# P times the softmax factors: one GpSimd instruction per attention step in place of four

## The chip, the core and the metric

The kernel runs on one core of a Trainium2 chip. A core has a matrix engine (TensorE, PE in the profile, with its weight loads as PEld), a vector engine (VectorE, DVE), an activation engine (ScalarE, ACT), a general engine (GpSimd, POOL), and SyncE (SP), which here only starts transfers. Each engine works through its own list of instructions in order; they wait for each other through semaphores. The metric is the device time in microseconds (us) of one execution.

## The reference

One layer of a streaming encoder, for 512 positions of width 1024, all in float32: a SwiGLU feed-forward block, a mixer with two branches (a gated linear recurrence, and attention in a sliding window), and a second feed-forward block, each between two RMS norms. What the change touches is the softmax of the attention, with 16 query heads in 4 groups of 4, and a learned sink per head that counts in the sum but has no value:

```
sc = einsum('bnqgrd,bnkgd->bngrqk', qc, kband) * HEAD_DIM ** -0.5
sc = sc + bias
sc = where(valid, sc, NEG_INF)
p  = softmax(concatenate([sc, sink], axis=-1), axis=-1)[..., :-1]
o  = einsum('bngrqk,bnkgd->bnqgrd', p, vband)
```

Everything after the projections of q, k and v and before the projection `w_attn_out` belongs to it. A query attends to its own chunk of 64 keys and to the two chunks before.

## The kernel before, in words

Every float32 product is made of three: operands are split into a high part that TensorE multiplies exactly enough (`whi`, `PH`, uT part 0) and a rest (`wlo`, `PL`, uT part 1), and high x high, rest x high and high x rest are added up in the accumulator. The splitting is work for ScalarE (high part, L178 and L213) and VectorE (rest, L179 and L214: a subtraction of 128x1024 elements for each block of weights, with both inputs in on-chip memory). Blocks of weights are loaded by SP in the order of one list (`order`), split a few blocks ahead, and used by `mm_feat` (L223 to L225), 24 matmuls a unit.

The order of the work is written out by hand. `mm_feat` calls `point()` twice a unit; `point()` counts up and emits what has come due, and `later(n, fn, rank)` puts a piece of work n points ahead. So the attention is woven between the units of matmuls in the stage from about 530 to 672 us: units of the q projection (`wq`), of the recurrent branch's output (`lru`) and of the gates (`wg`), listed in `att_units`.

There are 16 attention steps, 4 groups of heads `g` times 4 blocks of 128 queries `j`, started every 2.2 points (`ATT_STEP`). A step goes through five pieces, `ATT_LAG` points apart:

- `att_s` (L1292, L1293): TensorE makes the scores of four heads, 128 queries x 256 keys each (128 keys where j = 0).
- `scores` (L1298 to L1302): VectorE adds the bias, takes the row maximum, and writes the tile P (`pt`), 128 partitions (queries) x 4 heads x 256 columns.
- `exps` (L1306, L1307): ScalarE takes exponentials of P in place, one instruction a head, which also gives the sums `d`, 128x4; and the exponential of the sink.
- `factors` (L1309 to L1314): VectorE adds sink and sum and takes the reciprocal (L1310, L1311), so `d` holds a factor for each query and head; GpSimd multiplies P by it in place (L1313).
- `att_t` (L1329): TensorE transposes P, four blocks of 128x128 for j = 0 and eight otherwise, into PSUM (`pt`); ScalarE and VectorE split that into `PH` and `PL` (L213, L214); `att_o` (L1345, L1346) multiplies by v, and the output is put together by L1354 or L1356, L1360, L1364 and, on GpSimd, L1365.

Beside L1313 and L1365, GpSimd's list in this stage holds the loading of the bias tiles (L1274 to L1276) and, twice, the sums of weight blocks for the gates' last units (L543, L544, L538, L539), which use fewer products at the price of sums. The functions that the change touches:

Of the kernel before, what the change touches and what calls it, by code (L numbers as in the profile page):

```python
# [13 lines left out]
ALU = mybir.AluOpType  # L14

P = 128
# [35 lines left out]
def hybrid_layer(ctx: ExitStack, tc: tile.TileContext, a: dict, out: bass.AP):  # L52
    nc = tc.nc
    act, dve, pool, pe, sp = nc.scalar, nc.vector, nc.gpsimd, nc.tensor, nc.sync
# [8 lines left out]
    def slot(shape, dt=F32, name="s"):  # L63
        uid[0] += 1
        return sb.tile(shape, dt, tag="slot", name=f"{name}_{uid[0]}")

    def bank(name="ps"):
        uid[0] += 1
        return pp.tile([P, 512], F32, tag="ps", name=f"{name}_{uid[0]}")

    def small(w, name="m", bufs=4):
        uid[0] += 1
        return sm.tile([P, w], F32, tag=f"sm{w}", name=f"{name}_{uid[0]}", bufs={1: 11, 4: 12}.get(w, bufs))
# [123 lines left out]
    def later(n, fn, rank=1):  # L197
        uid[0] += 1
        due.append((now[0] + n, rank, uid[0], fn))
# [1078 lines left out]
    def att_s(g, j):  # L1278
        n = 256 if j else 128
        k0 = (j - 1) * P if j else 0  # L1280
        b0 = 256 - n
        pt = slot([P, 4, 256], name="P")
        m, ng, d, es = (small(4, x) for x in ("m", "ng", "d", "es"))
        sk = vec[:, V_SINK + 4 * g : V_SINK + 4 * g + 4]
        pss = []
        for hp in range(2):
            ps = bank("s")
            for hh in range(2):
                x = 2 * hp + hh
                o = ps[:, hh * 256 : hh * 256 + n]  # L1290
                lq = QS[2 * g + x // 2][:, x % 2, j * P : (j + 1) * P]
                pe.matmul(o, lq, KS[g][:, 0, k0 : k0 + n], start=True, stop=False)  # L1292
                pe.matmul(o, lq, KS[g][:, 1, k0 : k0 + n], start=False, stop=True)  # L1293
            pss.append(ps)

        def scores():
            for x in range(4):
                dve.tensor_tensor_reduce(  # L1298
                    out=pt[:, x, b0:256], in0=pss[x // 2][:, (x % 2) * 256 : (x % 2) * 256 + n], in1=BT[g][:, x, b0:256],
                    scale=1.0, scalar=sk[:, x : x + 1], op0=ALU.add, op1=ALU.max, accum_out=m[:, x : x + 1])  # L1300
            dve.tensor_scalar(out=ng, in0=m, scalar1=-1.0, scalar2=None, op0=ALU.mult)
            dve.tensor_tensor(out=es, in0=sk, in1=m, op=ALU.subtract)  # L1302

        def exps():
            for x in range(4):
                act.activation(pt[:, x, b0:256], pt[:, x, b0:256], AF.Exp, bias=ng[:, x : x + 1], accum_out=d[:, x : x + 1])  # L1306
            act.activation(es, es, AF.Exp)  # L1307

        def factors():  # L1309
            dve.tensor_tensor(out=d, in0=d, in1=es, op=ALU.add)  # L1310
            dve.reciprocal(d, d)  # L1311
            for x in range(4):
                pool.tensor_scalar(out=pt[:, x, b0:256], in0=pt[:, x, b0:256], scalar1=d[:, x : x + 1], scalar2=None, op0=ALU.mult)  # L1313
            at[(g, j)] = pt  # L1314

        later(ATT_LAG[0], scores, 0)
        later(ATT_LAG[0], exps, 2)
        later(ATT_LAG[1], factors, 3)
        later(ATT_LAG[2], lambda: att_t(g, j))

    def att_t(g, j):
        pt = at.pop((g, j))
        kts = (0, 1) if j else (1,)
        PH = slot([P, 2, 512], F32R, name="PH")
        PL = slot([P, 2, 512], F32R, name="PL")
        pss = [bank("pt") for _ in kts]
        for ps, kt in zip(pss, kts):
            for x in range(4):
                pe.transpose(ps[:, x * P : (x + 1) * P], pt[:, x, kt * P : (kt + 1) * P], ident)  # L1329
        def out():  # L1330
            for ps, kt in zip(pss, kts):
                split2(PH[:, kt, :], PL[:, kt, :], ps)

        later(ATT_LAG[3], out)
        later(ATT_LAG[4], lambda: att_o(g, j, PH, PL, kts))
# [217 lines left out]
```

## Time and profile before

| What | Value |
|---|---|
| Median of 3 runs | 1129.06 us (1128.47 to 1129.76) |
| Profiled execution | 1128.72 us, its span 1126.9 us |
| Granted TensorE clock | 0.999 |
| GpSimd busy | 369.0 us, 33% of the span |
| VectorE busy | 838.4 us, 74% |
| TensorE busy | 1117.2 us, 99% |

A row of a group of instructions names line, engine, operation, output<-inputs, shapes and count, then busy us and mean ns of one, then the idle time of the engine just before them with what ended it. A row of the order of time gives start (us from the span's start), length and the instruction, and in brackets the idle time before it and what ended that. A row of waits names the waiting instruction, the releaser, and us in total, times and the longest. In a row of one line's instructions stand the shortest, the median and the longest duration in ns, then the first and the last start. A row of busy time in a stretch gives for each engine busy us and, in brackets, the count of instructions. A profile records matmuls overlapping each other, since they are pipelined.

### The profile page before, as it was taken

The page shows a single profiled execution, that of the slowest core. Times are in us where ns is not written, and L with a number is a line of the kernel's source. Part 1 is how long each engine was busy: PE and PEld are TensorE (multiplying, and loading weights), DVE is VectorE, ACT ScalarE, POOL GpSimd, SP SyncE. Part 2 cuts the span into 40 slices and gives each one's busy share as a digit, 9 for nine tenths or more (in the row PEclk, how much of TensorE's full clock was granted, in tenths as well). Part 3 has the DMA queues.
Part 4 walks back from the last instruction along what each step waited for, and adds up shares of the span by engine and source line. Part 5 has one row for each costly group of instructions (what it writes and reads, how often), then busy time and mean ns, then how long its engine had stood idle before and what let it go on. Part 6 is the DMA issues. An engine that isn't in the chain of part 4 may idle for free.

```text
span 1126.9 us, 18141 instructions
## 1 busy us (share of the span) xinstructions
PE 1117.2 (99%) x7054; PEld 1012.9 (90%) x7054; DVE 838.4 (74%) x1238; ACT 623.4 (55%) x1114; POOL 369.0 (33%) x286
## 2 busy tenths in 40 slices
PE   9999999999999999999999999999999999999997
PEld 7899999988889977899888888889999999998886
DVE  5889989886436998887778877767898777975313
ACT  7755555574325778666656664456555555564211
POOL 0044444200000523242655863000966566700000
PEclk9999999999999999999999999999999999999999
DMA  9226563265314653156223235521333332255101
GB/s 337 108 82 149 136 129 113 76 224 168 98 53 148 157 118 102 38 171 241 60 91 113 92 134 186 211 90 38 113 107 92 102 113 86 88 199 170 40 19 56
DMA packets 40310, 136.54 MB, mean 121 GB/s; under 512 B 4880, under 2 KB 6800, under 8 KB 40224
## 3 DMA queue, kind: packets, MB, share of 16 engines
q1 hardware_dynamic: 36432, 123.28, 32.9%
q0 software_dynamic: 3504, 11.58, 5.3%
q8 instruction: 55, 0.90, 0.3%
q10 hardware_dynamic: 288, 0.52, 0.2%
q14 instruction: 31, 0.25, 0.1%
HBM read 121.74 MB, written 11.53 MB: 118 GB/s over the span
## 4 chain that ended last, share of the span: by engine, by line
PE 94%; DVE 2%; ACT 1%; POOL 1%; DMA 1%; issue 1%; DVEq 0%; SPq 0%; POOLq 0%; ACTq 0%
PE c L492 13%; PE c L493 13%; PE c L494 13%; PE acc L243 8%; PE acc L242 8%; PE acc L241 8%; PE f L223 8%; PE f L224 8%; PE f L225 8%; ACT P L1306 1%; DVE P L1298 1%; PE pt L1329 1%; PE tr L333 1%; DVE wlo L179 1%; PE f L849 1%
## 5 line engine op out<-in xcount | busy, mean ns | idle before, releaser
L492 PE MATMUL c<-uT,whi 128*128 128x256 f32 x528 | 149.8, 284 | 0.0
L494 PE MATMUL c<-uT,whi 128*128 128x256 f32 x528 | 149.7, 284 | 0.0
L493 PE MATMUL c<-uT,wlo 128*128 128x256 f32 x528 | 149.7, 283 | 0.0
L493 PE MATMUL c<-Xh,wlo 128*128 128x256 f32 x504 | 143.0, 284 | 0.0
L492 PE MATMUL c<-Xh,whi 128*128 128x256 f32 x504 | 143.0, 284 | 0.0
L241 PE MATMUL acc<-whi,hT 128*128 128x512 f32 x352 | 137.3, 390 | 0.0
L242 PE MATMUL acc<-wlo,hT 128*128 128x512 f32 x352 | 137.1, 390 | 0.0
L243 PE MATMUL acc<-whi,hT 128*128 128x512 f32 x352 | 137.1, 390 | 0.0
L223 PE MATMUL f<-uT,whi 128*128 128x512 f32 (+1 forms) x376 | 134.4, 358 | 0.0
L224 PE MATMUL f<-uT,wlo 128*128 128x512 f32 (+1 forms) x376 | 133.0, 354 | 0.0
L225 PE MATMUL f<-uT,whi 128*128 128x512 f32 (+1 forms) x376 | 133.0, 354 | 0.0
L214 DVE TENSOR_TENSOR wlo<-S,whi 128x1024 fp32r<-128x1024 f32 x88 | 129.1, 1466 | 5.1 <-ACT whi L213 4.2
L494 PE MATMUL c<-Xl,whi 128*128 128x256 f32 x456 | 129.3, 284 | 0.0
L213 ACT ACTIVATE whi<-S 128x1024 fp32r<-128x1024 f32 x88 | 90.4, 1054 | 25.8 <-DVE S L539 22.0
L493 PEld LDWEIGHTS c<-uT,wlo 128*128 128x128 f32 x528 | 101.5, 192 | 0.1
L492 PEld LDWEIGHTS c<-uT,whi 128*128 128x128 f32 x528 | 101.5, 192 | 0.1
L494 PEld LDWEIGHTS c<-uT,whi 128*128 128x128 f32 x528 | 101.5, 192 | 0.0
L492 PEld LDWEIGHTS c<-Xh,whi 128*128 128x128 f32 x504 | 96.9, 192 | 0.3 <-issue 0.3
L493 PEld LDWEIGHTS c<-Xh,wlo 128*128 128x128 f32 x504 | 96.9, 192 | 0.1
L494 PEld LDWEIGHTS c<-Xl,whi 128*128 128x128 f32 x456 | 87.7, 192 | 0.0
L223 PEld LDWEIGHTS f<-uT,whi 128*128 128x128 f32 x376 | 71.2, 189 | 10.9 <-issue 1.6
L225 PEld LDWEIGHTS f<-uT,whi 128*128 128x128 f32 x376 | 71.2, 189 | 9.8
(380 smaller groups left out, 2890.3 us busy)
## 6 DMA issues: line engine op xcount, KB each, us to landing
raw_w2a<-in_w2a_dram SPq DMA_DIRECT2D x22, 512.0 KB, 4.1
raw_w1b<-in_w1b_dram SPq DMA_DIRECT2D x22, 512.0 KB, 4.2
raw_w3b<-in_w3b_dram SPq DMA_DIRECT2D x22, 512.0 KB, 4.2
raw_w2b<-in_w2b_dram SPq DMA_DIRECT2D x22, 512.0 KB, 4.2
raw_w3a<-in_w3a_dram SPq DMA_DIRECT2D x21, 512.0 KB, 4.4
raw_w1a<-in_w1a_dram SPq DMA_DIRECT2D x20, 512.0 KB, 4.3
raw_wg<-in_wg_dram SPq DMA_DIRECT2D x16, 512.0 KB, 3.9
raw_xr<-in_xr_dram SPq DMA_DIRECT2D x8, 512.0 KB, 4.0
```

The source lines that it names most:

```text
L179: dve.tensor_tensor(out=lo, in0=r, in1=f32(hi), op=ALU.subtract)
L213: act.activation(hi, src, AF.Copy)
L214: dve.tensor_tensor(out=lo, in0=src, in1=f32(hi), op=ALU.subtract)
L223: pe.matmul(ps[:, c0:c1], wh[:, s], h_, start=k == 0, stop=False)
L224: pe.matmul(ps[:, c0:c1], wl[:, s], h_, start=False, stop=False)
L225: pe.matmul(ps[:, c0:c1], wh[:, s], l_, start=False, stop=k == KT - 1)
L241: pe.matmul(acc[n], x[:, 0, c], wh[:, s], start=first, stop=False)
L242: pe.matmul(acc[n], x[:, 0, c], wl[:, s], start=False, stop=False)
L243: pe.matmul(acc[n], x[:, 1, c], wh[:, s], start=False, stop=last)
L492: pe.matmul(ps, wh[:, s], xh, start=first, stop=False, skip_group_check=True)
L493: pe.matmul(ps, wl[:, s], xh, start=False, stop=False, skip_group_check=True)
L494: pe.matmul(ps, wh[:, s], xl, start=False, stop=k == 3, skip_group_check=True)
```

## The change

In `factors`, the loop of four GpSimd instructions, each of which multiplies one head's 128x256 (or 128x128) block by a column of `d`, is replaced by one two-operand multiplication over all four heads. Its second operand is `d` with a third dimension of step 0, so that each of a query's four factors is read again for each of the n columns of its head (n = 256, or 128 where j = 0). The multiplied numbers and their place are the same. The order of all instructions on the five engines stays, except that each group of four on GpSimd is now one, so 64 instructions become 16.

```diff
         def factors():
             dve.tensor_tensor(out=d, in0=d, in1=es, op=ALU.add)
             dve.reciprocal(d, d)
-            for x in range(4):
-                pool.tensor_scalar(out=pt[:, x, b0:256], in0=pt[:, x, b0:256], scalar1=d[:, x : x + 1], scalar2=None, op0=ALU.mult)
+            p_ = pt[:, :, b0:256]
+            pool.tensor_tensor(out=p_, in0=p_, in1=d.unsqueeze(2).to_broadcast([P, 4, n]), op=ALU.mult)
             at[(g, j)] = pt
```

A transpose on TensorE waits for the instruction on GpSimd that wrote its part of P: before, each head's transposes could start after that head's multiplication; now those of all four heads start after the one.

## The prediction

> **What bounds the kernel now.** I read the page first (busy shares, then the chain of work that ended last), then busy time by stretch for the attention stage, the waits in it, and the order of time of each engine there.
>
> ```profile
> PE 1117.2 (99%) x7054; PEld 1012.9 (90%) x7054; DVE 838.4 (74%) x1238; ACT 623.4 (55%) x1114; POOL 369.0 (33%) x286
> ...
> PE 94%; DVE 2%; ACT 1%; POOL 1%; DMA 1%; issue 1%; DVEq 0%; SPq 0%; POOLq 0%; ACTq 0%
> ```
>
> TensorE is busy for 1117.2 of 1126.9 us and carries 94% of the chain. GpSimd (POOL) carries 1%. The changed lines run only in the attention stage, from 530 to 672 us:
>
> ```profile
> core 0: us, PE busy (x) PEld busy (x) DVE busy (x) ACT busy (x) POOL busy (x), PEclk, DMA share, GB/s
> 530.00:672.00 142.00, 140.90 (x765) 121.20 (x764) 109.49 (x297) 87.26 (x233) 93.18 (x106) 1.00 0.31 97
> ```
>
> There TensorE stands idle 142.00 - 140.90 = 1.10 us at a granted clock of 1.00; VectorE (DVE) has 142.00 - 109.49 = 32.5 us to spare, GpSimd 48.8. So no more than about 1.1 us of visible idle time can be won in this stage. The waits say whose it is:
>
> ```profile
> POOL P L1313 <- DVE d L1311: 24.4, 8, 4.4
> ...
> DVE d L1310 <- ACT es L1307: 16.3, 12, 2.2
> ...
> PEld pt L1329 <- POOL P L1313: 1.5, 2, 0.8
> ...
> PE pt L1329 <- POOL P L1313: 1.1, 2, 0.6
> ```
>
> All of it, 1.1 us in two waits, is TensorE's transposes (L1329) waiting for the multiplications by the softmax factors (L1313). GpSimd itself mostly waits for VectorE's reciprocal (L1311). Each step's slack is the distance from the start of its multiplications on GpSimd to its first transpose on TensorE:
>
> ```profile
> 537.39 2.37 POOL L1313 TENSOR_SCALAR P<-P,d 128x128 f32<-128x128 f32 x4
> 543.11 4.67 POOL L1313 TENSOR_SCALAR P<-P,d 128x256 f32<-128x256 f32 x4 [3.35 <-ACT whi L178]
> 549.74 4.23 POOL L1313 TENSOR_SCALAR P<-P,d 128x256 f32<-128x256 f32 x4 [1.97 <-DVE d L1311]
> ...
> 632.33 4.59 POOL L1313 TENSOR_SCALAR P<-P,d 128x256 f32<-128x256 f32 x4
> ...
> 655.29 3.63 POOL L1313 TENSOR_SCALAR P<-P,d 128x256 f32<-128x256 f32 x4 [3.97 <-DVE d L1311]
> ...
> 664.82 4.70 POOL L1313 TENSOR_SCALAR P<-P,d 128x256 f32<-128x256 f32 x4
> ```
>
> ```profile
> 541.04 0.60 PE L1329 MATMUL pt<-ident,P 128*128 128x128 f32 x4
> ...
> 547.90 1.04 PE L1329 MATMUL pt<-ident,P 128*128 128x128 f32 x8
> ...
> 554.73 1.03 PE L1329 MATMUL pt<-ident,P 128*128 128x128 f32 x8
> ...
> 635.95 0.49 PE L1329 MATMUL pt<-ident,P 128*128 128x128 f32 x3
> 636.97 0.76 PE L1329 MATMUL pt<-ident,P 128*128 128x128 f32 x5 [0.53 <-POOL P L1313]
> ...
> 659.47 1.03 PE L1329 MATMUL pt<-ident,P 128*128 128x128 f32 x8
> ...
> 668.45 0.56 PE L1329 MATMUL pt<-ident,P 128*128 128x128 f32 x3
> 669.58 0.77 PE L1329 MATMUL pt<-ident,P 128*128 128x128 f32 x5 [0.57 <-POOL P L1313]
> ```
>
> The slacks are 3.65, 4.79, 4.99, 3.62, 4.18 and 3.63 us for the steps that start at 537, 543, 549, 632, 655 and 664 (the ten others have more). In the two that wait, TensorE did three transposes and stood before the fourth head's, for 0.53 and 0.57 us.
>
> **The change part by part.** *Removed:* 64 multiplications by a column of factors, four per step.
>
> ```profile
> L1313 POOL TENSOR_SCALAR P<-P,d 128x256 f32<-128x256 f32 x48 | 51.5, 1090 | 35.9 <-DVE d L1311 23.2 <-ACT PH L213 5.8 <-ACT es L1307 3.6
> ...
> L1313 POOL TENSOR_SCALAR P<-P,d 128x128 f32<-128x128 f32 x16 | 12.3, 778 | 1.3 <-DVE d L1311 1.2
> ```
>
> That is 51.5 + 12.3 = 63.8 us of GpSimd time: 12 full steps of about 4.3 us and four half-width ones of about 3.1 us.
>
> *Added:* 16 two-input multiplications, 12 of 128x1024 and 4 of 128x512 elements, whose second operand repeats one factor along 256 (or 128) columns. No row has such a repeated operand. The nearest are the two-input operations with plain operands:
>
> ```profile
> 636.88 0.72 POOL L1365 TENSOR_TENSOR OL<-o,OH 128x256 fp32r<-128x256 f32 x1
> ...
> 627.46 1.28 POOL L544 TENSOR_TENSOR S<-S,raw_wg 128x512 f32<-128x512 f32 x1
> ...
> L1170 POOL TENSOR_TENSOR xf<-xf,xf x4: 2412/3267/3279, 366.4 to 375.6; 128x1024 f32<-128x1024 f32 x4
> ...
> L544 POOL TENSOR_TENSOR S<-S,raw_w1a x8: 1622/2158/3448, 56.8 to 200.1; 128x512 f32<-128x512 f32 x8
> ...
> L176 POOL CAST whi<-raw_wg 128x1024 fp32r<-128x1024 f32 x6 | 6.8, 1257 | 22.5 <-PE i L1112 8.3 <-PE f L224 8.0 <-DVE xc_t L1128 6.2
> ```
>
> 0.72, 1.28 and 2.41 us for 256, 512 and 1024 elements lie on a line of 2.2 ns per element. I take 2.41 us for a full step and 1.28 for a half one, because shape, type and engine are the same and only the step of one operand differs. The lower end is a one-input pass over 128x1024, 1.26 us (if the repeated factor cost no reading); the upper end is twice the slowest two-input row of 128x512, 2 x 3.448 = 6.9 us. At my value GpSimd's work goes from 63.8 to 12 x 2.41 + 4 x 1.28 = 34.0 us, nearly all of it beside TensorE's work.
>
> The Trainium skill, "GPSIMD Engine Reference", section 4.1, speaks against the change: two-input elementwise work is about 2x slower than VectorE's there, while one-input work runs at roughly line rate. Estimated from its 1.2 GHz, four one-input passes of 256 columns would be 0.85 us, and its 2.6 cycles per element make one two-input pass of 1024 about 2.2 us, a loss of 1.4 us per step; 2.2 us is still under every slack, so the sum would be the same by it. The trace bears out the second figure and not the first: the fastest plain rows above are near 2.2 ns per element with two inputs, and the one-input multiplications average 1.09 us for 256.
>
> *Moved on the path.* TensorE's first transpose of a step used to need the first head only, now it needs all four; what counts is the slack against the single instruction. 2.41 is under every slack, by 1.21 us in the tightest step (3.62). Even if the instruction at 632 starts about 1 us late behind a VectorE operation, as the first of the four there did, 3.4 us is under 3.62. Both waits go: -0.53 - 0.57 = -1.10 us. What is late next in these two steps is TensorE's own queue.
>
> *Nothing new is queued in front of others:* order and count of GpSimd's other instructions, of its bias loads and of SP's transfers stay. Behind the multiplication on GpSimd stand the subtractions of L1365 and the weight sums of L538 to L544; they start up to 2 us earlier, which frees ScalarE's buffers sooner, worth nothing while TensorE has no other idle time in the stage. The adding up of the sums and the reciprocal (L1310, L1311) stay on VectorE at no change.
>
> *The price on VectorE.* A long two-input GpSimd instruction and a VectorE operation with two SBUF inputs do not run together:
>
> ```profile
> 366.38 12.46 POOL L1170 TENSOR_TENSOR xf<-xf,xf 128x1024 f32<-128x1024 f32 x4 [11.82 <-ACT xf L350]
> ```
>
> ```profile
> 373.15 3.42 DVE L1059 TENSOR_TENSOR rglo<-rgraw,rghi 128x1024 fp32r<-128x1024 f32 x1
> ...
> 550.15 1.23 DVE L179 TENSOR_TENSOR wlo<-raw_wq,whi 128x1024 fp32r<-128x1024 f32 x1 [0.58 <-ACT whi L178]
> ...
> 578.52 1.23 DVE L179 TENSOR_TENSOR wlo<-raw_lru,whi 128x1024 fp32r<-128x1024 f32 x1 [0.63 <-ACT whi L178]
> ...
> L179 DVE TENSOR_TENSOR wlo<-raw_lru,whi x7: 1214/1226/1227, 535.4 to 610.6; 128x1024 fp32r<-128x1024 f32 x7
> L179 DVE TENSOR_TENSOR wlo<-raw_wq,whi x5: 1218/1226/1227, 530.1 to 587.7; 128x1024 fp32r<-128x1024 f32 x5
> L179 DVE TENSOR_TENSOR wlo<-raw_wg,whi x4: 1218/1442/2310, 614.5 to 640.2; 128x1024 fp32r<-128x1024 f32 x4
> ```
>
> Beside L1170 a subtraction of 128x1024 takes 3.42 us; beside the four short multiplications (550.15 lies inside the series 549.74 to 553.97) it takes its plain 1.23 and the series is stretched instead. With one instruction of 2.41 us from 549.74 the subtraction of 550.15 would wait until 552.15, 2.0 us. There are 16 such subtractions in the stage. I take nine as held for 2.0 us, 18 us of VectorE time against 32.5 us to spare, about 2 per step, so I cost it at nothing for TensorE. The cover is VectorE's idle time; if it is gone, what follows is the second rival. Ends: 0 held, and all 16 by 3.42 - 1.23 = 2.2, 35 us.
>
> **The sum:** 1128.72 - 1.10 = 1127.6 us, against the profiled execution's own time (1128.72, of which 1126.9 are its span); this execution lies 0.34 us under the median of the runs shown, 1129.06. The case's own range is 1127.2 to 1129.5: the lower end adds that the weight loads waited 1.5 us, 0.4 more than the matmuls, the upper end lets the held VectorE operations bring back about 2 us. 0.2%, 2.26 us, is about what a measurement of this kernel can tell from no change.
>
> **Rivals.** *1. The repeated operand is read slowly (slower).* For it: no row shows it, and worst two-input rows run at 6.7 ns per element. Against it: the line of 2.2 ns through three sizes. With D the length of a full-width instruction, TensorE waits max(0, D - slack) in the steps at 543, 549, 632, 655 and 664. At D = 4.9: 0.11 + 0 + 1.28 + 0.72 + 1.27 = 3.4, less the 1.10 won, +2.3; from there it decides. At D = 6.0: 1.21 + 1.01 + 2.38 + 1.82 + 2.37 = 8.8, +7.7, 1136.4 us, or more, since steps of longer slack are left out. At 6.9 the same sum gives 13.3, +12.2, 1140.9 us.
>
> *2. VectorE held for the whole instruction becomes the bound (slower).* For it: 3.42 against 1.23 above, and from 0 to 35 us of holding against 32.5 us of spare time. Against it: in 12 of the 16 steps VectorE waits for ScalarE's last exponentials before L1310 (16.3 us), and can catch up there. If a third of the 18 us is not caught up, 6 us arrive at the transposes: 1127.6 + 6 = 1133.6 us. It decides once 3.4 us arrive. The Trainium skill, "SBUF — State Buffer", section "Who interferes with whom", states the same as a rule: the pair of ports that VectorE shares with GpSimd is an exclusive lock, held for a whole instruction, and a VectorE instruction with two SBUF inputs contends with a GpSimd one that reads SBUF. The rows of L1170 and L1059 agree; the short multiplications, beside which the subtraction kept its 1.23 us, do not show the block.
>
> *3. No gain: the two waits stay.* Step 632 starts behind a weight sum and a VectorE operation; if the instruction runs at 3.27 us, as three of the four of L1170 did, and 1 us late, it ends at 636.6, and TensorE waits as before: 1128.7 us.
>
> *4. More than the waits is won* (1126.0 us): GpSimd free 30 us sooner would have to speed up work outside the two waits, of which the idle time of TensorE in this stage shows none.
>
> **How the numbers follow.** Forecast 0.44, rival 3 0.13, together the same (within 0.2%): 0.57. Rival 1 0.20, rival 2 0.17: slower 0.37. Rival 4 0.06: faster. The likeliest is 1127.6. The range goes down to 1126.3, which leaves out 0.06, and up to 1136.4 (rival 2 whole, rival 1 up to D = 6.0), which leaves out about 0.13.
>
> **What would show it.** Right: L1313 with 16 rows of TENSOR_TENSOR, about 2.4 to 3.3 us at full width, GpSimd's busy time in the stage 25 to 30 us less, no wait of L1329 for L1313, and the subtractions of L179 longer, some near 3.2 us, with VectorE's busy time in the stage up by 10 to 20 us. Wrong: rows of 4.9 us and more with TensorE waiting at the five tight steps (rival 1), or L1313 short and late, with VectorE near 100% and TensorE waiting for it (rival 2).

## The result and the profile after

The changed kernel takes 1136.49 us (median of 6 runs, 1135.57 to 1137.18) against 1129.2 us before (6 runs, 1128.47 to 1130.08): the ratio is 1.0064, with a 95% interval of 1.0053 to 1.0075. It is slower by 0.64%. The profiled execution took 1136.02 us, its span 1134.2 us, 7.3 us more than the span before.

Busy time of the engines, from the page, then the stretch from 530 to 680 us, for the changed kernel (columns as before):

```profile
PE 1120.4 (99%) x7054; PEld 1013.5 (89%) x7054; DVE 848.0 (75%) x1238; ACT 623.5 (55%) x1114; POOL 337.9 (30%) x238
```

```profile
530.00:680.00 150.00, 144.22 (x772) 121.95 (x771) 120.74 (x299) 88.07 (x234) 63.18 (x58) 1.00 0.29 93
```

The same stretch of the kernel before:

```profile
530.00:680.00 150.00, 148.90 (x828) 129.03 (x827) 115.19 (x306) 94.08 (x246) 95.09 (x107) 1.00 0.33 103
```

GpSimd's work did shrink, by 369.0 - 337.9 = 31.1 us over the kernel. But in the same 150 us TensorE stood idle for 5.8 us in place of 1.1, and VectorE was busy for longer while it finished less. The multiplications in order of time on GpSimd, the first three of full width and the last, after the change:

```profile
543.00 1.89 POOL L1313 TENSOR_TENSOR P<-P,d 128x1024 f32<-128x1024 f32 x1 [4.93 <-DVE d L1311]
...
551.51 1.90 POOL L1313 TENSOR_TENSOR P<-P,d 128x1024 f32<-128x1024 f32 x1 [6.62 <-DVE d L1311]
560.64 1.89 POOL L1313 TENSOR_TENSOR P<-P,d 128x1024 f32<-128x1024 f32 x1 [7.24 <-DVE d L1311]
...
672.08 1.89 POOL L1313 TENSOR_TENSOR P<-P,d 128x1024 f32<-128x1024 f32 x1 [0.38 <-ACT PH L213]
```

An instruction of 1024 elements takes 1.89 us, less than half of the four that it replaces. Yet the second one starts at 551.51, where its series started at 549.74 before, and the last at 672.08 in place of 664.82: +1.8, then +7.3 us, which is the whole loss. GpSimd is early done and waits longer for the next factors. What makes them late is seen on VectorE, in order of time and by line, after the change:

```profile
543.34 2.63 DVE L179 TENSOR_TENSOR wlo<-raw_wq,whi 128x1024 fp32r<-128x1024 f32 x1 [0.57 <-ACT whi L178]
...
551.65 2.83 DVE L179 TENSOR_TENSOR wlo<-raw_wq,whi 128x1024 fp32r<-128x1024 f32 x1 [0.57 <-ACT whi L178]
...
561.08 2.53 DVE L179 TENSOR_TENSOR wlo<-raw_lru,whi 128x1024 fp32r<-128x1024 f32 x1 [0.57 <-ACT whi L178]
```

```profile
L179 DVE TENSOR_TENSOR wlo<-raw_lru,whi x7: 1216/2533/2575, 535.6 to 617.4; 128x1024 fp32r<-128x1024 f32 x7
L179 DVE TENSOR_TENSOR wlo<-raw_wq,whi x5: 1216/2571/2835, 530.3 to 592.4; 128x1024 fp32r<-128x1024 f32 x5
L179 DVE TENSOR_TENSOR wlo<-raw_wg,whi x4: 1217/1529/2909, 622.7 to 648.7; 128x1024 fp32r<-128x1024 f32 x4
```

The weight subtraction that starts 0.34 us after the multiplication (543.34 against 543.00) takes 2.63 us in place of 1.23: it ends 1.08 us after the multiplication's end (545.97 against 544.89), as if all but 0.15 us of it had run from there. The medians of the first two groups doubled. The waits of the changed kernel between 530 and 690 us:

```profile
POOL P L1313 <- DVE d L1311: 58.0, 11, 7.2
...
DVE d L1310 <- ACT es L1307: 16.0, 12, 2.2
...
PE f L223 <- DVE o L1360: 3.2, 2, 2.4
...
PE pt L1329 <- DVE QS L1250: 1.0, 1, 1.0
```

TensorE no longer waits for P anywhere. It waits above all for VectorE, and for instructions whose output it does not read at that place: f (L223) does not use what L1360 writes, nor the transposes what L1250 writes. Both instructions of VectorE read a bank of PSUM, the memory into which TensorE writes; the kernel takes all its banks from one pool of eight. In the program that the changed kernel compiles to, the f that starts at 564.52 is written into the bank that L1360 has just read, the transposes at 556.04 into the one that L1250 has just read, and a wait for that read stands in front of each. So TensorE waits for a bank that late VectorE has not yet read out. L1360's last read of that bank and the f that takes the bank over, in the kernel before:

```profile
559.12 0.84 DVE L1360 TENSOR_TENSOR o<-o,o 64x256 f32<-64x256 f32 x2
```

```profile
560.17 0.40 PE L223 MATMUL f<-uT,whi 128*128 128x512 f32 x1
```

And in the changed kernel:

```profile
563.54 0.83 DVE L1360 TENSOR_TENSOR o<-o,o 64x256 f32<-64x256 f32 x2
```

```profile
564.52 0.47 PE L223 MATMUL f<-uT,whi 128*128 128x512 f32 x1 [2.38 <-DVE o L1360]
```

Before, f starts 0.21 us after the read has ended (560.17 against 559.96), without any wait. After, it starts 0.15 us behind the read and has waited 2.38 us for it.

### The profile page after: what moved, and what is told of

It reads as the page before. It is cut to its first block, busy times and chain, and to the rows that moved or that the text cites. A ratio compares the mean times of both kernels' runs of the same rounds, so it can differ in the third digit from the quotient of the medians.

```text
span 1134.2 us, 18095 instructions
## 1 busy us (share of the span) xinstructions
PE 1120.4 (99%) x7054; PEld 1013.5 (89%) x7054; DVE 848.0 (75%) x1238; ACT 623.5 (55%) x1114; POOL 337.9 (30%) x238
## 5 line engine op out<-in xcount | busy, mean ns | idle before, releaser
L223 PE MATMUL f<-uT,whi 128*128 128x512 f32 (+1 forms) x376 | 134.5, 358 | 2.4 <-DVE o L1360 2.4
L223 PEld LDWEIGHTS f<-uT,whi 128*128 128x128 f32 x376 | 71.2, 189 | 13.8 <-issue 4.2
```

What stands on the lines that cost most here:

```text
L223: pe.matmul(ps[:, c0:c1], wh[:, s], h_, start=k == 0, stop=False)
```

## The experiments

The theory after the result: the multiplication, being one long instruction with two inputs, holds VectorE's subtraction with two on-chip inputs until it ends; VectorE runs late, and TensorE waits for VectorE. The rivals: that all transposes now wait for one instruction, or that the kind of instruction (two inputs, a repeated operand) costs the time at any length.

**The same instruction, started later.** A small copy, which waits for the reciprocal, and three small memsets stand in front of it on GpSimd, so that VectorE's subtraction comes first:

```diff
+            pool.tensor_copy(gap[:, :4], d)
+            for q in range(3):
+                pool.memset(gap[:, 8:168], 0.0)
             pool.tensor_tensor(out=p_, in0=p_, in1=d.unsqueeze(2).to_broadcast([P, 4, n]), op=ALU.mult)
```

> The single GpSimd multiplication stays, but starts some 0.7 us later after the factors are ready: a copy of the 128x4 factors and three small memsets stand in front of it on GpSimd, so that VectorE's weight subtraction (L179), which follows the reciprocal, starts first. Theory (the long two-input instruction holds VectorE's subtraction when it starts first): the subtractions that took about 2.6 us are back at 1.23, TensorE's waits for PSUM banks go, 1127 to 1130 us. Rival (the four heads' common wait, or the instruction's own kind, costs the time): the multiplication now ends later still, so 1136 us or more.

Measured: 1127.26 us, ratio 0.9979 to the kernel before (0.9969 to 0.9988). GpSimd, then VectorE in order of time, then the stretch from 530 to 680 us:

```profile
542.79 0.19 POOL L1313 COPY gap<-d 128x4 f32<-128x4 f32 x1 [3.75 <-DVE d L1311]
542.91 0.81 POOL L1315 MEMSET gap<- 128x160 f32 x3
543.69 2.23 POOL L1316 TENSOR_TENSOR P<-P,d 128x1024 f32<-128x1024 f32 x1
```

```profile
542.94 1.23 DVE L179 TENSOR_TENSOR wlo<-raw_wq,whi 128x1024 fp32r<-128x1024 f32 x1 [0.57 <-ACT whi L178]
```

```profile
530.00:680.00 150.00, 150.00 (x842) 130.66 (x842) 117.23 (x309) 94.10 (x246) 80.32 (x123) 1.00 0.34 106
```

The subtraction started first and kept its 1.23 us; the multiplication was stretched instead, to 2.23 us, and ended at 545.92, 1.0 us later than in the changed kernel. TensorE has no idle time left in the stretch. Delaying the multiplication took the ratio from 1.0064 to 0.9979: the common wait of the four heads cannot be the cause, and this version beats both kernels.

**Smaller pieces of the same kind.** Four instructions a step, one a head, or two, each of two heads:

```diff
-            pool.tensor_tensor(out=p_, in0=p_, in1=d.unsqueeze(2).to_broadcast([P, 4, n]), op=ALU.mult)
+            for x in range(4):
+                pool.tensor_tensor(out=p_[:, x], in0=p_[:, x], in1=d[:, x : x + 1].to_broadcast([P, n]), op=ALU.mult)
```

```diff
+            for x in (0, 2):
+                pool.tensor_tensor(out=p_[:, x : x + 2], in0=p_[:, x : x + 2], in1=d[:, x : x + 2].unsqueeze(2).to_broadcast([P, 2, n]), op=ALU.mult)
```

> Four two-input multiplications per step, one a head, each with that head's factor repeated by a step of 0, in place of the one over four heads. Theory (what matters is how long one instruction holds the port): a subtraction on VectorE is held for at most one piece of about 0.5 us, mean of L179 below 1.7 us, 1128 to 1131 us. Rival (two inputs or the repeated operand are the cause at any length): L179 at about 2.6 us at the same places and 1135 to 1138 us.

> Two multiplications per step, each over two heads with the repeated operand. Theory (length of one hold): a piece of about 1 us holds a subtraction by at most 0.6 us, half of what the whole one does, 1129 to 1133 us. Rival (kind, not length): 1135 to 1138 us.

Measured: with four 1127.71 us, ratio 0.9981 (0.9972 to 0.9991), which is under the range that the theory gave; with two 1129.49 us, ratio 0.9998 (0.9988 to 1.0007). The subtractions of the lru blocks, first with four pieces, then with two:

```profile
L179 DVE TENSOR_TENSOR wlo<-raw_lru,whi x7: 1215/1255/1298, 535.5 to 609.9; 128x1024 fp32r<-128x1024 f32 x7
```

```profile
L179 DVE TENSOR_TENSOR wlo<-raw_lru,whi x7: 1215/1679/1723, 535.7 to 612.2; 128x1024 fp32r<-128x1024 f32 x7
```

The medians go 1.26, 1.68, 2.53 us for four, two and one instruction a step, and the times 1127.7, 1129.5, 1136.5 us. Among two-input multiplications, what counts is how long one instruction is: two inputs and the repeated operand do no harm in short pieces. The kind counts too, though: a two-input piece of two heads took 1.04 us and held the subtraction by 0.45 us, while the one-input multiplications of the kernel before took 0.92 us and did not hold it. How a long one-input instruction would do, no run shows.

**VectorE late without any long instruction.** The kernel before, with the subtraction done twice on VectorE for eight blocks that were held:

```diff
+HELD = {("wq", 4), ("wq", 5), ("lru", 2), ("lru", 4), ("wq", 7), ("lru", 5), ("lru", 7), ("wg", 10)}
...
                 dve.tensor_tensor(out=lo, in0=r, in1=f32(hi), op=ALU.subtract)
+                if order[k] in HELD:
+                    dve.tensor_tensor(out=lo, in0=r, in1=f32(hi), op=ALU.subtract)
```

> The kernel before, with its four one-input multiplications a step, but VectorE does the weight subtraction twice for the eight blocks that were held longest in the changed kernel (wq 4, 5, 7; lru 2, 4, 5, 7; wg 10): 8 x 1.23 = 9.8 us more on VectorE at the same places, with no long instruction on GpSimd. Theory (the time is lost because VectorE is late and returns PSUM banks late): 1132 to 1137 us, with TensorE waiting for VectorE at f and pt. Rival (VectorE has 32 us to spare and catches up, the loss comes from the multiplication itself): 1128 to 1130 us.

Measured: 1138.38 us, ratio 1.0082 (1.0067 to 1.0097), a little above the range. TensorE's waits in order of time, in this kernel and then in the changed one (the last column is the wait and what ended it; lines are 2 higher in the first):

```profile
556.28 0.63 PE L1331 MATMUL pt<-ident,P 128*128 128x128 f32 x4 [0.70 <-DVE QS L1252]
...
564.88 0.47 PE L225 MATMUL f<-uT,whi 128*128 128x512 f32 x1 [2.51 <-DVE o L1362]
```

```profile
556.04 0.63 PE L1329 MATMUL pt<-ident,P 128*128 128x128 f32 x4 [0.95 <-DVE QS L1250]
...
564.52 0.47 PE L223 MATMUL f<-uT,whi 128*128 128x512 f32 x1 [2.38 <-DVE o L1360]
```

They are the same two waits at the same places, without any change to the multiplications. The eight repeats added 11.0 us on VectorE (1.30 to 1.38 us each), somewhat more than planned. VectorE's lateness is enough to explain the loss.

**The same instruction, with the held subtractions taken from VectorE.** In the changed kernel GpSimd does the subtraction of the same eight blocks:

```diff
-                dve.tensor_tensor(out=lo, in0=r, in1=f32(hi), op=ALU.subtract)
+                (pool if order[k] in HELD else dve).tensor_tensor(out=lo, in0=r, in1=f32(hi), op=ALU.subtract)
```

> The changed kernel, with the eight weight subtractions that were held (wq 4, 5, 7; lru 2, 4, 5, 7; wg 10) moved from VectorE to GpSimd, behind the multiplication there. Theory (TensorE waits for PSUM banks that VectorE frees late because it is held): VectorE loses 8 x 2.6 us, TensorE's waits go, 1127 to 1129 us. Rival (the single multiplication makes the transposes late): 1134 us or more, since GpSimd has more to do.

Measured: 1127.45 us, ratio 0.9981 (0.9972 to 0.9991). The stretch, and GpSimd's subtractions:

```profile
530.00:680.00 150.00, 150.00 (x842) 130.60 (x841) 111.82 (x302) 94.14 (x246) 80.64 (x67) 1.00 0.34 106
```

```profile
L179 POOL TENSOR_TENSOR wlo<-raw_lru,whi x4: 2395/2402/2414, 559.5 to 612.2; 128x1024 fp32r<-128x1024 f32 x4
```

TensorE is again never idle, though GpSimd has 17 us more to do than in the changed kernel. The changed kernel itself, on the same chip, came out at 1136.53 us, ratio 1.0061 (1.0046 to 1.0076), as it was expected to:

> The changed kernel as it is, on the same chip as the other kernels of this call: 1.005 to 1.008 of the time before by either theory.

**Another second operand, and another engine.** First the multiplication with P itself as second operand, which leaves out the factors; then the multiplication on VectorE:

```diff
+            pool.tensor_copy(gap[:, :4], d)
+            pool.tensor_tensor(out=p_, in0=p_, in1=p_, op=ALU.mult)
```

```diff
+            dve.tensor_tensor(out=p_, in0=p_, in1=d.unsqueeze(2).to_broadcast([P, 4, n]), op=ALU.mult)
```

> The single GpSimd multiplication over four heads has P itself as second operand, 1024 different elements, in place of the factors repeated by a step of 0 (a copy of the 128x4 factors in front keeps the wait for the reciprocal); the output is then not the softmax, since the squares of the exponentials take the place of the products. Theory (what costs is the time that a two-input instruction reads through the shared port): a plain second operand is read longer, the row is near 2.41 us in place of 1.89, L179 held to 2.9 us or more, 1136 to 1142 us. Rival (the repeated operand is the cause): L179 back near 1.23 us and 1128 to 1131 us.

> VectorE itself does the one multiplication a step, GpSimd none. VectorE's plain two-input rows of 128x1024 take 1.23 us, so this adds some 12 x 1.23 + 4 x 0.69 = 17.5 us to VectorE with no hold. Theory (late VectorE returns PSUM banks late, whatever makes it late): slower than before, 1135 to 1145 us, with TensorE waiting for VectorE. Rival (the hold between two engines is what hurts, not VectorE's time): 1127 to 1130 us.

Measured: 1136.61 us, ratio 1.0063 (1.0048 to 1.0078), and 1135.28 us, ratio 1.005 (1.0033 to 1.0067). The groups of the multiplication and of a subtraction in the first, and the stretch in the second:

```profile
L1314 POOL TENSOR_TENSOR P<-P 128x1024 f32<-128x1024 f32 x12 | 23.7, 1978 | 0.0
```

```profile
L179 DVE TENSOR_TENSOR wlo<-raw_wq,whi x5: 1215/2705/2707, 530.1 to 592.4; 128x1024 fp32r<-128x1024 f32 x5
```

```profile
530.00:680.00 150.00, 145.57 (x793) 124.47 (x791) 128.24 (x318) 90.45 (x239) 31.89 (x42) 1.00 0.31 99
```

A second operand without the step of 0 gives the same time, so the repeated operand is not the cause; that it would be read for 2.41 us was a miss (1.98 on average, as with the factors). And with the multiplication on VectorE, no multiplication on GpSimd can hold a subtraction, but VectorE is busy for 128 of 150 us and the kernel is slower again: time added to VectorE in this stage costs, however it gets there. It does not always cost the same: the multiplications took 18.4 us on VectorE and cost 5.6 us, a smaller share than in the other runs, and why is not shown.

**Is it the PSUM banks?** The scores of the four half-width steps in one bank in place of two, in the changed kernel and in the kernel before:

```diff
-        for hp in range(2):
+        nh = 2 if j else 4
+        for hp in range(4 // nh):
             ps = bank("s")
-            for hh in range(2):
-                x = 2 * hp + hh
-                o = ps[:, hh * 256 : hh * 256 + n]
+            for hh in range(nh):
+                x = nh * hp + hh
+                o = ps[:, hh * n : hh * n + n]
```

> The changed kernel, with the scores of the four half-width steps (j = 0, four heads of 128 columns) in one PSUM bank in place of two; everything else is as it was, VectorE is held as before. Theory (TensorE waits because banks come back late from VectorE): with one bank less in use in four of sixteen steps, part of the waits go, 1132 to 1135.5 us. Rival (TensorE waits for the values that VectorE writes, not for the banks): no change, 1136 to 1137 us.

> The kernel before with the same one bank in place of two in the half-width steps: by either theory within 0.2% of the time before, since TensorE waits for no bank there.

Measured: 1136.32 us, ratio 1.0061 (1.0044 to 1.0078), and 1129.76 us, ratio 1.0001 (0.9992 to 1.0011). The changed kernel with this edit, its waits between 530 and 690 us:

```profile
PE s L1293 <- DVE g L1265: 1.2, 1, 1.2
PE pt L1330 <- DVE m L1299: 1.1, 4, 0.5
PE pt L1330 <- DVE QS L1250: 1.0, 1, 1.0
PE f L223 <- DVE o L1361: 0.8, 1, 0.8
```

The waits of f fell from 3.2 to 0.8 us, since f now goes into another bank, but others took their place, all for VectorE, and no time was won. So the theory of the banks, as I had sized it, missed: TensorE does stop at a bank each time, as the compiled program shows, but with one bank less in use in four steps it stops at the next one, because VectorE is as late as before.

## Why the prediction was wrong

*Bound, and the two waits for P: right.* TensorE bounds the kernel, and the single instruction ends well inside every slack. No wait of a transpose for P is left. Where nothing else gets in the way, the 1.10 us and a little more are won: spans of 1125.1 and 1125.4 us (started later, and subtractions moved) against 1126.9.

*Length of the instruction: mis-sized, and harmless.* I took 2.41 us, it took 1.89. The rival of a slowly read operand, for which I kept the most room among the slower cases, was wrong: D never came near 4.9 us. One slack was misread: the half-width step that starts at 604 had 4.41 us, less than two of the six that I listed; as the sums for D take full-width steps alone, none of them changes. That the upper end of my range, 1136.4 us, lies so close to the measured 1136.49 is luck, since it was worked out from that rival at D = 6.0.

*The hold on VectorE: the mechanism was right.* I had 2.0 us for nine subtractions, 18 us. Eight of the 16 were held, for 1.3 to 1.7 us (the medians and maxima of L179's rows against 1.22), 11.4 us in all. One of them had been held by 1.1 us before, behind a weight sum (the 2310 ns in the row of `raw_wg` in the prediction), so 10.3 us are new. VectorE was busy for 120.74 - 115.19 = 5.6 us more in the same stretch, although it finished less there. The shorter instruction made the hold shorter than I had it.

*The cover: this is the step that failed.* "18 us of VectorE time against 32.5 us to spare, about 2 per step, so I cost it at nothing for TensorE." Of the 10.3 us of new holds 7.3 us arrived in the span, and eight subtractions done twice, 11.0 us, cost about 9 us of the whole kernel: little was absorbed. The first three holds (543.34, 551.65, 561.08) are 1.40 + 1.60 + 1.30 = 4.3 us, and the L1360 behind them is 4.42 us later than before (563.54 against 559.12), 0.2 us of which were there before the first hold (535.6 against 535.4 in L179's rows): up to there next to nothing was caught up. The 32.5 us are not spare. Half of them, 16.3 us, is VectorE waiting for ScalarE's exponentials before L1310, and after the change the same wait is still there at 16.0 us: a step goes VectorE, ScalarE, VectorE, GpSimd, TensorE, and the idle time is part of that chain. A VectorE that comes late to the scores makes the exponentials late and waits just as long for them. I had cited that very wait as the place where it would catch up.

*Who waits for VectorE: left out.* I measured slack from the multiplication to the transposes only, and asked whether P would be late. TensorE stopped elsewhere, at f and pt, for VectorE's reading of other results (L1360, L1250). The tightest slack that I had was 3.62 us; the f at 560.17 had 0.21 us behind the read of its bank, so it could hide next to nothing of the first three holds. The second rival held this mechanism with a chance of 0.17 and 1133.6 us, on the guess that a third of the hold would not be caught up; 7.3 of 10.3 us were not. The sign that I named for it, VectorE near 100%, did not come: it was busy for 120.74 of 150 us, 80%, and TensorE waited for it all the same. What should have changed the chance is the slack of 0.21 us above. The chain of work that ended last in the kernel before, asked for the stretch from 610 to 672 us alone, points the same way (its shares by line; TensorE, with 94% of the whole chain, is not among the largest here):

```profile
by line: ACT P L1306 12.8%; DVE P L1298 11.9%; DVE wlo L179 10.2%; POOL P L1313 9.1%; issue 8.1%; DMA Xb<-t_scr 5.1%; ACT whi L213 4.9%; DVE ng L1301 4.1%; DVE PL L214 3.1%; DVE wlo L214 2.4%; POOL S L544 2.1%; POOL S L538 2.1%; POOL S L543
```

VectorE and ScalarE lead it, L179 among the first: the page's 94% is an average over stages, and in this one a late VectorE stood close behind TensorE. It would have told only a part: up to 612 us the chain runs over TensorE alone, and 6.0 of the 7.3 us were lost by then (the f that starts at 605.82 before starts at 611.82 after).

The rule of the Trainium skill, "SBUF — State Buffer", section "Who interferes with whom", that the first to start takes the shared ports for its whole instruction, agrees with both orders seen here: multiplication first, and the subtraction took 2.63 us; subtraction first (started-later kernel), and it took 1.23 while the multiplication took 2.23 in place of 1.89. It does not fit the one-input multiplications of the kernel before, which start first and read P: the subtraction beside them kept its 1.23 us, and the series of four was stretched instead (4.23 us at 549.74, against 4 x 0.92).

## What to carry to other kernels

Before a short series of GpSimd instructions is made into one, look at what VectorE starts within its length: if the one instruction has two inputs, a two-input VectorE operation that starts within it waits for its end, where short pieces let it in; four two-input pieces, or the same instruction started 0.9 us after the factors were ready, kept the gain. Idle time of an engine is cover only if what ends the idle time does not move with that engine's own lateness: check the releaser, and look whether it stands behind the same engine. And a slack has to be taken from every consumer of the delayed engine, those that wait for a buffer to be read out among them, not from the one consumer of the changed instruction.

## What the runs showed of the hardware that I had not expected

- A GpSimd multiplication of 128x1024 float32 elements with two inputs took 1.89 us, with the second input repeated or not; subtractions of the same size took 2.41 (L1170 before) and 2.40 us (the weight subtractions moved to GpSimd). The runs do not tell apart the operation, the number of different tiles read and the output's type.
- The one-input multiplications of 128x256, 0.92 us each, did not hold VectorE's subtraction at all (1.23 us beside them), while four two-input ones, 0.61 us each, held it by only 0.03 us in the median and one of 1024 elements by 1.3. The hold by a two-input instruction was what was left of that instruction when the subtraction started, less 0.15 us: 1.40 of 1.55 us at 543.34 and 1.60 of 1.76 us at 551.65 in the changed kernel.
- A memset on GpSimd beside the subtraction did not hold it (1.23 us beside the memsets at 542.91).
